# A routed expert FFN with run-time branches: more branches announced ahead, group work moved inside the arms, a one-hot made before the branch

## The chip, the core and the metric

The kernel runs on one core of a Trainium2 chip. The metric is the device time of one execution in microseconds (us), the median of three runs. TensorE (PE) does the matrix products, VectorE (DVE) and ScalarE (ACT) the element-wise work, and SyncE (SP) starts the loads of the expert weights.

## What is computed

One encoder layer over 256 tokens and 16 meta tokens of width 1024: two token mixers, a LayerNorm, then a feed-forward part in which each of the 256 tokens goes to 4 of 32 experts, then a LayerNorm. The change lies in the expert part alone:

```
def moe_ffn(x, ...):
    logits = x @ w_router + b_router
    top_val, top_idx = top_k(logits, 4)
    gates = softmax(top_val)
    # for each expert e, over the tokens that chose it:
    hidden = xb @ w_gate_up[e] + b_gate_up[e]            # 1024 -> 2048
    gate, up = hidden[:, :1024], hidden[:, 1024:]
    gate, up = minimum(gate, 7), clip(up, -7, 7)
    y = (gate * sigmoid(1.702 * gate) * (up + 1)) @ w_down[e] + b_down[e]
    # out[token] = sum over its 4 experts of gate_of_expert * y
```

How many tokens an expert gets is known only at run time.

## The kernel before

The mixers take the first 380 us or so. Then come the 32 experts in order, written out one behind the other in the program. The weights of an expert are 12 pages of 1 MB each, 8 of `w_gate_up` and 4 of `w_down`. They go through a ring of 19 buffers; SP starts the load of the page 19 places further on as soon as PE has used a page (`follow`), so a stall of PE ahead of such a use also delays a load.

An expert's work depends on its number of tokens n, which each engine loads into a register (`counts`). Three branches choose the arm: the outer one, labelled `x{e}` (n > 32), the inner one (n > 64), and inside that n > 96.

- The **small arm** (n up to 32): one part A, that is 8 steps of up products (L1098, with the bias at L1096), the activation on DVE and ACT (`act`, L1103 to L1111), two transposes (`turn`, L1117), 4 steps of down products (L1130), and the copy of the result into `yrow` (`place`, L1138 and L1140). 20 experts take it.
- The **mid arm** (33 to 64): parts A and B side by side. Seven experts take it: 7, 8, 14, 23, 25, 27 and 29.
- The **far arm** (65 and more): first `pick` makes a one-hot `eo` of the tokens past 64 (L1045), `gather` and `slots` use it (L1070, L1078, L1080), then come A and B and the further parts C and D. Experts 4, 6, 11, 20 and 30 take it.

In the program of PE an expert stands as: outer branch, inner branch, far arm, mid arm, small arm; behind the small arm is the place where all arms meet, called the landing here. The small arm runs straight into it; the far and the mid arm jump over what stands between. Behind the landing PE loads the next count (L1183) and comes to the next outer branch (L1192) and inner branch (L1193).

The tokens of four consecutive experts (a group, `GE` = 4) are gathered together. Between the landing of a group's last expert (e = 3, 7, 11, ...) and the next outer branch stand, in straight code, `gather_group` (L1055), and twice a `combine` (L1169, the previous group's rows into the sums `acc`) and a `slots` (L1078, L1080).

`tell` announces on PE the coming outer branch: an instruction that names the branch and says whether n > 32 there. It stands at the start of the small and the mid arm and behind the ups of A and B in the far arm.

## Time and profile before

| what | value |
|---|---|
| median of three runs | 1482.67 us (1479.99 to 1483.79) |
| the profiled execution, its own time | 1474.79 us |
| its span, first to last instruction | 1472.7 us |
| PE busy, share of the span | 1185.7 us, 81% |
| mean granted TensorE clock | 0.908 of full speed |
| DMA read over the span | 454.27 MB |

The profiled execution is 2.1 us longer than its span, and it is 0.5% below the median of the three runs. Times in the rows are counted from the start of the span; the expert part runs from about 381 us on. In a timeline row the first number is the start, the second the duration of a run of equal instructions, and the bracket at the end the idle time of the engine before them with what ended it; "issue" there means that no other engine or transfer that the profile shows ended it.

### The profile page before, as it was taken

To read this page: it belongs to the slowest core of one execution; us is meant where nothing else is said; L and a number is where in the kernel's file an instruction comes from. 1 tells how busy PE (TensorE), PEld (TensorE's weight loads), DVE (VectorE), ACT (ScalarE), POOL (GpSimd) and SP (SyncE) were. 2 spreads that over 40 slices of the span, in tenths; PEclk is the share of its full clock that TensorE was granted. 3 is DMA by queue.
4 is the path that set the end of the run, shared out by engine and by line. 5 is a ranking of instruction groups with operands and counts; after the bars stand their busy time and mean duration, and the time that the engine had idled before them with its cause. 6 is when DMAs were issued, how large, how long until landed. Compare 5 with 4: busy or idle time off the path is not lost. (4 is left out here: it accounts for less than half of the span.)

```text
span 1472.7 us, 24271 instructions
## 1 busy us (share of the span) xinstructions
PE 1185.7 (81%) x10294; PEld 727.6 (49%) x10294; DVE 426.1 (29%) x940; ACT 294.6 (20%) x630; POOL 83.0 (6%) x65
## 2 busy tenths in 40 slices
PE   5899999899777968688697976856976777787875
PEld 5799999889532533344243533411532443242432
DVE  5976765456411110211112012011021111111113
ACT  4454475454300100001000100100100010010011
POOL 5422400000100000000000000000000000000001
PEclk9999999999888999989888889977898898899888
DMA  6465673768499998877998399999998999999740
GB/s 170 133 168 125 153 185 106 225 200 332 182 405 417 418 412 354 347 301 302 377 418 325 151 416 418 415 418 418 419 382 350 416 417 416 417 416 414 307 174 31
DMA packets 101982, 458.40 MB, mean 311 GB/s; under 512 B 8626, under 2 KB 49739, under 8 KB 52635
## 3 DMA queue, kind: packets, MB, share of 16 engines
q1 hardware_dynamic: 100554, 451.59, 79.2%
q0 software_dynamic: 800, 3.03, 0.7%
q8 instruction: 146, 2.39, 0.7%
q10 hardware_dynamic: 400, 0.73, 0.2%
q14 instruction: 82, 0.66, 0.1%
HBM read 454.27 MB, written 1.05 MB: 309 GB/s over the span
## 5 line engine op out<-in xcount | busy, mean ns | idle before, releaser
L1098 PE MATMUL pA<-ring,w 128*32 128x512 f32 x2048 | 294.3, 664 | 21.7 <-DMA ring<-in_w_gate_up_dram 21.1
L1098 PEld LDWEIGHTS pA<-ring,w 128*32 128x32 f32 x2048 | 91.9, 120 | 170.9 <-issue 112.4
L1130 PE MATMUL dA<-ring,hd 128*32 128x256 f32 x2048 | 150.9, 443 | 17.4 <-ACT hd L1118 14.5
L1103 DVE TENSOR_SCALAR hd<-pA 128x256 f32<-128x256 f32 x32 | 13.6, 425 | 449.5 <-PE pA L1098 322.2
L1098 PE MATMUL pB<-ring,w 128*32 128x512 f32 x768 | 116.2, 618 | 0.0
L1130 PEld LDWEIGHTS dA<-ring,hd 128*32 128x32 f32 x2048 | 72.3, 126 | 79.8 <-issue 26.0
L1105 ACT ACTIVATE thA<-hd 128x256 f32<-128x256 f32 x32 | 13.3, 416 | 468.6 <-DVE hd L1103 455.0
L1140 DVE COPY yrow<-dA 32x256 f32<-32x256 f32 x96 | 40.4, 420 | 216.1 <-PE dA L1130 153.5
L1096 PE MATMUL pA<-bgt,sel 96*32 96x256 bf16 x256 | 19.4, 337 | 99.6 <-issue 93.2
L1096 PEld LDWEIGHTS <-sel 96*32 96x32 bf16 x400 | 12.8, 104 | 138.5 <-issue 124.5
L1055 PE MATMUL xg<-ext,hh 128*128 128x256 f32 x256 | 63.5, 410 | 8.7 <-issue 4.5
L1055 PEld LDWEIGHTS xg<-ext,hh 128*128 128x128 f32 x256 | 52.1, 206 | 21.2 <-issue 7.8
L1169 PE MATMUL acc<-yrow,pgb 128*128 128x512 f32 x128 | 58.1, 598 | 1.0 <-DVE yrow L1140 1.0
L1245 POOL DMA_DIRECT2D ring<-in_ln_g_dram x1 | 0.6, 574 | 1018.5 <-PE dB L1130 1018.5
L1098 PEld LDWEIGHTS pB<-ring,w 128*32 128x32 f32 x768 | 33.0, 116 | 46.9 <-issue 46.8
L1117 PE MATMUL atA<-ident,hd 128*128 128x128 f32 x64 | 16.0, 334 | 47.4 <-DVE hd L1111 47.4
L1138 ACT COPY yrow<-dA 32x256 f32<-32x256 f32 x32 | 11.6, 363 | 200.2 <-DVE yrow L1140 153.9
L1130 PE MATMUL dB<-ring,hd 128*32 128x256 f32 x768 | 51.6, 387 | 0.0
L1117 PEld LDWEIGHTS atA<-ident,hd 128*128 128x128 f32 x64 | 10.1, 207 | 78.2 <-issue 61.5
L1098 PE MATMUL pC<-ring,ext 128*32 128x512 f32 x320 | 39.7, 612 | 0.6 <-issue 0.6
L162 PE MATMUL xbc<-hTh,wh_xbc 128*128 128x272 f32 x128 | 38.2, 300 | 0.0
L163 PE MATMUL xbc<-hTl,wh_xbc 128*128 128x272 f32 x128 | 37.8, 296 | 0.0
(523 smaller groups left out, 2120.3 us busy)
## 6 DMA issues: line engine op xcount, KB each, us to landing
ring<-in_w_gate_up_dram SPq DMA_DIRECT2D x256, 1024.0 KB, 19.9
ring<-in_w_down_dram SPq DMA_DIRECT2D x127, 1024.0 KB, 19.5
wr_xbc<-in_w_in_dram SPq DMA_DIRECT2D x8, 1024.0 KB, 10.5
wr_g<-in_w_in_dram SPq DMA_DIRECT2D x8, 1024.0 KB
wr_z<-in_w_in_dram SPq DMA_DIRECT2D x4, 1024.0 KB
wr_k<-in_w_in_dram SPq DMA_DIRECT2D x4, 1024.0 KB, 10.9
wr_v<-in_w_in_dram SPq DMA_DIRECT2D x4, 1024.0 KB
wr_q<-in_w_in_dram SPq DMA_DIRECT2D x4, 1024.0 KB, 13.7
```

Source lines behind the costliest of these rows:

```text
L162: TE.matmul(p, wh, xh, start=first, stop=False)
L163: TE.matmul(p, wh, xl, start=False, stop=False)
L1055: TE.matmul(p[:, j, :], h1[:, b, k * 128:(k + 1) * 128], oh[:, b, :], start=b == 0, stop=b == 1)
L1096: TE.matmul(o[:, u, :], sel[:, e:e + 1].to_broadcast([96, 32]), bgt[u][:, 256 * j:256 * j + 256], start=u == 0, stop=False)
L1098: TE.matmul(o, x[:, k, :], w[:, :, 256 * j:256 * j + 256], start=False, stop=k == KD - 1)
L1103: V.tensor_scalar(gg, p[:, 0, :], 7.0, None, ALU.min)
L1105: A.activation(t, gg, AF.Tanh, scale=0.851)
L1117: TE.transpose(p[:, t, :], hd[:, co + 256 + t:co + 512:2], ident)
L1130: TE.matmul(p[j * 32:(j + 1) * 32, :], at[:, t, k * 32:(k + 1) * 32], w[:, t, j * 256:(j + 1) * 256], start=k == 0 and t == 0, stop=k == 3 ...
L1138: A.copy(o, p[r0:r0 + 32, :])
L1140: V.tensor_copy(o, p[j * 32:j * 32 + 32, :])
L1169: TE.matmul(ap[b][n], w[b], y[:, n * 512:(n + 1) * 512], start=False, stop=stop)
```

## The change

- A table `mid` holds for each expert 1 if n is up to 32 or over 64 and 0 from 33 to 64. Five DVE operations make it once, and PE loads an entry of it for each expert beside the count (L1182).
- The inner branch gets a label, `y{e}`, and `tell` announces it too, behind the outer one, with that entry as its direction. A third branch `z{e}` with an empty body is put at the landing and is named by `tell(True)` in the far and the mid arm. Its condition is `nz > S` with nz at most 1, so it can never hold, and the built program has neither this branch nor an announcement of it: PE has 186 announcements where there were 93, two in each place instead of one.
- `fill` puts the group work inside the arms, between ups and downs: both `combine` and `slots` into the group's first expert, `gather_group` into its last. Each arm has a copy of its own.
- `pick(e, 64)` runs ahead of the outer branch for every expert, and `eo` gets a fixed place in the tail of the buffer of `w1`.
- A second definition of `wps` with the same text is removed. Lines of the operations shift: downs from L1130 to L1127, `combine` from L1169 to L1166.

```
-        eo = wk.tile([128, NB, 64], F32, tag="sd", name=f"eo{name}")
         for b in range(NB):
             V.tensor_scalar(eo[:, b, :], iota[:, 0:64], float(off), posm[:, b, e:e + 1], ALU.add, ALU.is_equal)
-        return eo
...
+        pick(e, 64)
         with tc.If(n > 32, label=f"x{e}") as c1:
-            with tc.If(n > 64) as c2:
-                eo = pick(e, 64, f"{e}")
+            with tc.If(n > 64, label=f"y{e}") as c2:
                 gather(eo, f"x{e}")
                 slots(eo, slice(e, e + 1), pgx, f"x{e}")
                 ups(e, [pa, pb_], False)
-                tell()
+                tell(True)
...
             with c2.Else():
-                tell()
+                tell(True)
                 ups(e, [pa, pb_], True)
-                mark()
+                fill()
                 downs(e, [pa, pb_], True)
         with c1.Else():
-            tell()
+            tell(False)
             ups(e, [pa], True)
-            mark()
+            fill()
             downs(e, [pa], True)
+        with tc.If(nz > S, label=f"z{e}"):
+            pass
...
-            def mark(m=m, e=e):
+            def fill(e=e, g=g, el=el):
                 if e == 0:
                     start_acc()
                     V.memset(yx, 0.0)
+                if el == 0:
+                    for i in range(2):
+                        if e:
+                            combine(pgb[i], yrow[:, i])
+                        slots(oh[:, :, 128 * i:128 * i + 128], slice(g * GE, (g + 1) * GE), pgb[i], f"{'AB'[i]}{g}")
+                if el == GE - 1 and e + 1 < NE:
+                    gather_group(f"{g + 1}", range(0, 8, 2))
 
-            def tell(m=m, e=e):
+            def tell(far, m=m, e=e):
+                if far:
+                    tc.mark_branch_hint_location(f"z{e}", engines=[ET.PE])
                 if m is not None:
-                    tc.mark_branch_hint_location(f"x{e + 1}", hint=m > 32, engines=[ET.PE])
-
-            arms(e, n, mark, tell)
-            if el == GE - 1 and e + 1 < NE:
-                gather_group(f"{g + 1}", range(0, 8, 2))
-            if el == GE - 1 and e + 1 < NE or e == 0:
-                for i in range(2):
-                    if e:
-                        combine(pgb[i], yrow[:, i])
-                    h = g + 1 if e else 0
-                    slots(oh[:, :, 128 * i:128 * i + 128], slice(h * GE, (h + 1) * GE), pgb[i], f"{'AB'[i]}{h}")
+                    tc.mark_branch_hint_location(f"x{e + 1}", hint=m[0] > 32, engines=[ET.PE])
+                    tc.mark_branch_hint_location(f"y{e + 1}", hint=m[1], engines=[ET.PE])
```

On PE, at the border of experts 23 and 24, the program before has this behind the last downs (`dA`) of expert 23's small arm; the landing is the row behind the first branch:

```order
L1130 MATMUL dA_25726<-ring_3896,hd 32x256 x8
L1192 UNCONDITIONAL_BRANCH
L1055 MATMUL xg_25767<-ext,hh 128x256 x4
L1055 MATMUL xg_25773<-ext,hh 128x256 x4
L1055 MATMUL xg_25779<-ext,hh 128x256 x4
L1055 MATMUL xg_25785<-ext,hh 128x256 x4
L1169 MATMUL acc_3888<-yrow,pgb_3883 128x512
...
L1080 MATMUL ptB_25809<-gth,ext 128x4 x2
L1183 TENSOR_LOAD cnt
L1192 COMPARE_AND_BRANCH
L1193 COMPARE_AND_BRANCH
```

The changed kernel has at the same place, from the last ups of that arm on:

```order
L1098 MATMUL pA_26955<-ring_3933,w_3882 32x512 x4
L1055 MATMUL xg_27010<-ext,hh 128x256 x4
L1055 MATMUL xg_27016<-ext,hh 128x256 x4
L1055 MATMUL xg_27022<-ext,hh 128x256 x4
L1055 MATMUL xg_27028<-ext,hh 128x256 x4
L1117 MATMUL atA_27034<-ident,hd 128x128 x2
...
L1192 UNCONDITIONAL_BRANCH
L1181 TENSOR_LOAD cnt
L1182 TENSOR_LOAD mid
L1182 ISA x2
L1192 COMPARE_AND_BRANCH
L1193 COMPARE_AND_BRANCH
```

The gather stands between ups and transposes now, the `combine` rows have gone on into expert 24, and between the landing and the two branches only loads are left.

On DVE, ahead of the same two branches of expert 24, the program before has:

```order
L1183 TENSOR_LOAD cnt
L1192 COMPARE_AND_BRANCH
L1193 COMPARE_AND_BRANCH
L1045 TENSOR_SCALAR eo_25834<-iota,posm 128x64 x2
L1086 COPY gslx_25860<-ptx_25855 64x1
```

and the changed kernel:

```order
L1181 TENSOR_LOAD cnt
L1046 TENSOR_SCALAR w_3882<-iota,posm 128x64 x2
L1192 COMPARE_AND_BRANCH
L1193 COMPARE_AND_BRANCH
L1086 COPY gslx_27130<-ptx_27125 64x1
```

The two operations of `pick` moved from the far arm to a place ahead of both branches, and write into the buffer `w`.

## Rows read from the trace of the kernel before

**Rows 1.** Windows of the expert part; GB/s last, DMA share before it, granted clock before that

```profile
540.00:832.00 292.00, 229.98 (x2184) 112.60 (x2180) 44.38 (x123) 25.37 (x65) 0.00 (x0) 0.89 0.80 323
832.00:1032.00 200.00, 144.13 (x1278) 58.95 (x1274) 26.59 (x72) 13.59 (x34) 0.00 (x0) 0.85 1.00 414
1032.00:1472.00 440.00, 332.86 (x3064) 164.62 (x3052) 72.50 (x192) 43.44 (x101) 5.27 (x5) 0.89 0.85 347
```

**Rows 2.** Waits of PE over the span: total us, times, longest us

```profile
PE pA L1096 <- issue: 93.2, 16, 10.6
PE atA L1117 <- DVE hd L1111: 47.4, 26, 2.9
PE xgx L1070 <- DVE eo L1045: 10.4, 5, 3.1
```

**Rows 3.** Timeline of PE, where it last waits for pages, and of SP's page loads

```profile
467.13 1.94 PE L1098 MATMUL pA<-ring,w 128*32 128x512 f32 x8 [1.42 <-DMA ring<-in_w_gate_up_dram]
1031.62 1.07 PE L1130 MATMUL dA<-ring,hd 128*32 128x256 f32 x16 [0.76 <-DMA ring<-in_w_down_dram]
800.13 32.34 SPq L1002 DMA_DIRECT2D ring<-in_w_gate_up_dram  x3
```

**Rows 4.** The inner branch on PE's sequencer: ns min/median/max

```profile
L1193 PEldq COMPARE_BRANCH  x24: 65/3741/6758, 489.3 to 1422.1; - x24
```

**Rows 5.** Timeline of PE: first instruction of expert 10 and of experts 23, 27, 29, 7

```profile
725.45 0.47 PE L1096 MATMUL pA<-bgt,sel 96*32 96x256 bf16 x8 [0.58 <-DVE yrow L1140]
1149.68 0.68 PE L1096 MATMUL pA<-bgt,sel 96*32 96x256 bf16 x8 [5.64 <-issue]
1272.69 0.68 PE L1096 MATMUL pA<-bgt,sel 96*32 96x256 bf16 x8 [5.97 <-issue]
1344.38 0.68 PE L1096 MATMUL pA<-bgt,sel 96*32 96x256 bf16 x8 [5.70 <-issue]
630.01 0.68 PE L1096 MATMUL pA<-bgt,sel 96*32 96x256 bf16 x8 [10.63 <-issue]
```

**Rows 6.** Timeline of PE behind landings reached by a jump

```profile
706.80 0.68 PE L1096 MATMUL pA<-bgt,sel 96*32 96x256 bf16 x8 [9.12 <-issue]
1111.06 0.68 PE L1096 MATMUL pA<-bgt,sel 96*32 96x256 bf16 x8 [9.62 <-issue]
657.58 7.17 PE L1055 MATMUL xg<-ext,hh 128*128 128x256 f32 x32 [1.03 <-ACT yrow L1138]
805.70 7.16 PE L1169 MATMUL acc<-ext,pgx 64*128 64x512 f32 x8 [3.91 <-issue]
1182.74 5.23 PE L1055 MATMUL xg<-ext,hh 128*128 128x256 f32 x23 [1.30 <-issue]
1306.54 8.40 PE L1055 MATMUL xg<-ext,hh 128*128 128x256 f32 x31 [3.21 <-issue]
```

**Rows 7.** Timeline of PE: activation waits of a small and a mid arm

```profile
1137.71 0.48 PE L1117 MATMUL atA<-ident,hd 128*128 128x128 f32 x2 [2.04 <-DVE hd L1111]
1138.69 5.35 PE L1130 MATMUL dA<-ring,hd 128*32 128x256 f32 x64 [0.51 <-ACT hd L1118]
1167.39 0.48 PE L1117 MATMUL atA<-ident,hd 128*128 128x128 f32 x2 [1.14 <-DVE hd L1111]
1168.95 0.51 PE L1117 MATMUL atB<-ident,hd 128*128 128x128 f32 x2 [1.08 <-DVE hd L1111]
```

**Rows 8.** Timeline of PE ahead of expert 12, and ups at two clocks

```profile
822.46 3.60 PE L1169 MATMUL acc<-yrow,pgb 128*128 128x512 f32 x8
830.65 0.43 PE L1096 MATMUL pA<-bgt,sel 96*32 96x256 bf16 x8
725.66 7.12 PE L1098 MATMUL pA<-ring,w 128*32 128x512 f32 x64
707.18 9.67 PE L1098 MATMUL pA<-ring,w 128*32 128x512 f32 x64
```

**Rows 9.** The load of a count on PE's sequencer: ns min/median/max

```profile
L1183 PEldq TENSOR_LOAD <-cnt x32: 297/304/487, 388.0 to 1370.2; - x32
```

## The prediction

> **What bounds the kernel now.** I began with windows of the expert part, because the change touches nothing ahead of it but some small front work. The reader is to see three stretches [rows 1]. From 540 to 832 us the DMA engines are busy for 0.80 of the time and move 323 GB/s: the ring is full, loads wait for PE to use a page, and PE sets the pace. From 832 to 1032 the share is 1.00 at 414 GB/s: the loads set the pace. From 1032 on it is 0.85 at 347 GB/s, and PE sets the pace again. The timeline agrees: PE waits for pages around 467 us, and the last such wait ends at 1031.62; SP's three loads from 800.13 on stretch over 32.34 us, so the loads stop there until PE goes on [rows 3]. The path that sets the end is therefore PE from about 467 to 832, the loads from 832 to 1032, and PE from 1032 to the end. A microsecond saved on PE counts in the first and the last of these, and not in the middle.

> Next I read what PE waits for [rows 2]. By far the most stands at its first instruction of an expert (L1096): 93.2 us in 16 waits that nothing visible ended ("issue"). Behind that come 47.4 us ahead of the transposes, where PE waits for the activation, and 10.4 us in five waits for the one-hot of the far arm. These three are what the change is about.

> The 93.2 us look like code that isn't there yet when a branch lands. The inner branch is short at best, 65 ns, but its median is 3741 ns and its maximum 6758 ns [rows 4]. The outer branch is announced before: from small expert 9 to small expert 10 the jump goes over two whole arms and costs 0.58 us. Where the same small landing leads to a mid expert, the inner branch, not announced, jumps, and PE stands for 5.64, 5.97 and 5.70 us [rows 5]. Where the landing was itself reached by a jump, out of a mid or far arm, PE stands for 9.12 and 9.62 us although the outer branch had been announced [rows 6]: one fetch for the landing, one more for the arm.

> **The change part by part.**

> *Inner branch announced.* Experts 23, 27 and 29 are mid experts behind a small one in the last stretch: 5.64 + 5.97 + 5.70, each down to 0.58, saves 15.6 us [rows 5]. Expert 25 is alike, but its predecessor is the first of a group and its arm grows by the `combine` work between announcement and use; I count it at nothing, and at 5 more as the bound. Expert 7 follows a far expert and waits 10.63 us against 9.62 for a small expert in the same position [rows 5, 6], so its inner branch adds about 1.0 there: -1.0. Expert 14 lies in the stretch of the loads: nothing. The nothing-bound for all of this is rival C.

> *Landing announced.* The built program has no third announcement, so the jumps into the landing cost what they did.

> *Group work leaves the landing.* This speaks against the change. Behind the jump out of the last expert of a group stood straight code on PE, a gather of 7.17 us and the combines, under which the fetch of the next arm was hidden: ahead of experts 8, 12, 24 and 28 PE stood only 1.03, 3.91, 1.03 + 1.30 and 1.03 + 3.21 us (the 1.03 of the later two is the same wait as at 657.58) [rows 6]. Now two branches follow the landing at once, as they do at the 9.12 and 9.62 us. I take 9.12 behind the mid arms (7, 23, 27) and 9.62 behind the far arm (11): +8.1, +5.7, +6.8, +4.9 = +25.5 us. If only one fetch of 5.64 were exposed, it would be +11; with 10.63 at each, +31.

> [...]

> *Group work covers the activation.* In a small arm PE waits 2.04 us ahead of the transposes and 0.51 behind them, in a mid arm 1.14 and 1.08 [rows 7]. A gather or a combine of several us now lies in that place, on PE, while DVE and ACT finish. In the stretches that count these are experts 3, 19, 24 and 28 (small, 2.55 each) and 7, 8, 23 and 27 (mid, 2.22 each): -19.1 us. Far arms hide nearly all of it already behind their second half, and I count them at nothing. If DVE and ACT were held up by the copies and `slots` that come along, part of this would come back; the bound is half, +9.5.

> *One-hot ahead of the branch.* Five waits, 10.4 us [rows 2], all of them far experts in the stretches that count: -10.4. The two DVE operations run for every expert now, but DVE is busy for 44.38 of 292 us [rows 1], and reaches the landing ahead of PE. If `eo` in the buffer of `w1` waited for the previous users, that would be far experts' work long done: nothing.

> *Loads restart earlier.* `combine` and `slots` stand ahead of expert 12's ups from 822.46 to 830.65 us [rows 8], and the loads stand still meanwhile [rows 3]. Behind the ups they no longer delay the release of pages: -8.2, at the start of the stretch that the loads set.

> *Small things.* Another load of a register per landing, 0.304 us [rows 9], at some 21 landings that count: +6.4 if none is hidden; with the five small operations in front I take +6. The copies lengthen the code of all arms, so straight code crosses into code not yet there somewhat oftener: I choose +2, from one to two crossings of the 1.30 us that one cost inside a gather [rows 6].

> The clock: ups behind a long stall ran 9.67 us, without one 7.12 [rows 8], so 2.5 us hang on each stall. Three or four stalls vanish and four appear, so nothing is left.

> Sum: -15.6 - 1.0 + 25.5 - 19.1 - 10.4 - 8.2 + 6 + 2 = -20.8 us. The profiled execution took 1474.79, which makes 1454; it was itself 0.5% below the median of 1482.67, so the median after is forecast as 1482.67 - 20.8 = 1462.

> **The rivals.**

> *B, slower: the second announcement wipes out the first.* The two branches stand next to each other, and the trace of before never has two announcements open at once, so nothing there says that both are kept. If the later one wins, announced jumps to small arms behind small arms become full stalls: experts 10 and 22 lose 5.64 - 0.58 + 2.5 of clock = 7.6 us each, and 1, 2 and 3 as much again, of which I count half, since the ring hides some there: 15.2 + 11.4 = +26.6. The time is 1462 + 26.6 = 1488. For it: the announced gain is one of a single prefetch. Against it: an announcement names its own branch. It decides when these losses exceed 25 us.

> *C, no change: the inner announcement has no effect,* because it comes too late behind the first or because the outer branch's outcome supersedes it. The 16.6 us stay: 1462 + 16.6 = 1479. For it: the landing's jump already undoes an announced outer branch [rows 6]. Against it: behind a small arm there is no jump.

> *D: PE's gains end in page waits.* After 1032 the loads run at 0.85 share, so 15% of 440 us, 66 us, are spare [rows 1], against some 16 us net gained there (15.6 and 12.1 of covered activations and 4.1 of one-hots, less 11.7 at the landings of 24 and 28 and 4 of small things). I give it no more than a few us in the range.

> **How the numbers follow.** The forecast has 0.55, B 0.27, C 0.13, all else 0.05. Its own range is 1442 (the landing's lower bound, -14.5, and expert 25's 5) to 1474 (the upper bound +5.5 and a third of the uncovered activations). The range that should hold the time 8 times in 10 reaches on to B: 1442 to 1489. A measurement here can tell about 0.3%, 4.4 us, from no change: 0.53 of the forecast and half of C are faster, 0.60 in all; the other half of C, a third of B and the rest are the same, 0.18; the rest of B and mishaps are slower, 0.22.

> **What would show it.** Gaps under 1 us ahead of experts 23, 27 and 29 show the inner announcement right; 9 us ahead of 8, 12, 24 and 28 show the exposed landings; no wait for the activation in experts 3, 7, 8, 19, 23, 24, 27 and 28; no wait for `eo` at all; loads that restart some 8 us sooner behind expert 11. Stalls of 5 us ahead of experts 1, 2, 3, 10 and 22 would show B; unchanged stalls at 23, 27 and 29 show C. The forecast is most easily wrong in the landings: if the exposed stalls are as short as 5 us, the gain is nearly double; if the outer announcement fails at more places, it is gone.

## The result and the profile after

The changed kernel took 1526.45 us (median of 4 runs, 1520.13 to 1534.17) against 1482.73 us; the ratio is 1.031, with a 95% interval from 1.027 to 1.035. It is slower by 3.1%, where 1.4% faster was forecast and 1489 was the upper end of the range. The profiled execution has a span of 1529.7 us, so 57.0 us more than the one of before; that one was 8 us below its kernel's median and this one is 5 us above, so some 13 of the 57 are the choice of the two executions.

The waits of PE over the span, largest first (total us, times, longest):

```profile
PE pA L1096 <- issue: 167.9, 23, 12.5
PE atA L1117 <- DVE hd L1111: 28.7, 15, 3.0
PE dA L1127 <- ACT hd L1118: 13.8, 22, 0.9
PE xgx L1070 <- DVE w L1046: 12.0, 5, 3.1
PE pA L1098 <- issue: 9.0, 4, 3.9
```

Beside [rows 2]: the stalls ahead of an expert's first instruction grew from 93.2 us in 16 to 167.9 in 23, the wait for the activation fell from 47.4 to 28.7, the wait for the one-hot did not fall (10.4 to 12.0), and a wait is there that was not among the larger ones: stalls inside straight code of the ups, 9.0 us. Waits for pages are gone from the list; before, it had this:

```profile
PE pA L1098 <- DMA ring<-in_w_gate_up_dram: 21.1, 21, 1.5
```

The timeline of PE, first instruction of an expert; here small experts behind small ones (1, 2, 3, 10, 17, 22):

```profile
440.07 0.68 PE L1096 MATMUL pA<-bgt,sel 96*32 96x256 bf16 x8 [6.38 <-issue]
464.40 0.68 PE L1096 MATMUL pA<-bgt,sel 96*32 96x256 bf16 x8 [6.56 <-issue]
488.13 0.68 PE L1096 MATMUL pA<-bgt,sel 96*32 96x256 bf16 x8 [6.46 <-issue]
771.43 0.68 PE L1096 MATMUL pA<-bgt,sel 96*32 96x256 bf16 x8 [6.39 <-issue]
1010.49 0.68 PE L1096 MATMUL pA<-bgt,sel 96*32 96x256 bf16 x8 [7.85 <-issue]
1177.46 0.68 PE L1096 MATMUL pA<-bgt,sel 96*32 96x256 bf16 x8 [6.23 <-issue]
```

Each of them stands for 6 us and more; expert 10 waited 0.58 before [rows 5]. Mid experts behind small ones (14, 23, 29), and experts behind a group's end (8, 24, 28):

```profile
919.25 0.47 PE L1096 MATMUL pA<-bgt,sel 96*32 96x256 bf16 x8 [0.81 <-DVE yrow L1137]
1199.27 0.47 PE L1096 MATMUL pA<-bgt,sel 96*32 96x256 bf16 x8 [0.77 <-DVE yrow L1137]
1396.70 0.47 PE L1096 MATMUL pA<-bgt,sel 96*32 96x256 bf16 x8 [0.73 <-ACT yrow L1135]
...
704.08 0.68 PE L1096 MATMUL pA<-bgt,sel 96*32 96x256 bf16 x8 [7.93 <-issue]
1241.58 0.68 PE L1096 MATMUL pA<-bgt,sel 96*32 96x256 bf16 x8 [12.53 <-issue]
1374.17 0.68 PE L1096 MATMUL pA<-bgt,sel 96*32 96x256 bf16 x8 [9.85 <-issue]
```

The announced inner branch works: 23 and 29 waited 5.64 and 5.70 us before [rows 5], 0.77 and 0.73 now. The landings at a group's end are exposed as forecast ahead of 8, 24 and 28; ahead of 12 PE stands 3.19 us, where 9.62 was taken. The picture is that of rival B: mid experts behind small ones no longer stall, small ones do.

What ends such a stall can be read from the traces of both kernels. Transfers of the kind "instruction" have a queue of their own there (packets, MB, share), before and after:

```profile
q8 instruction: 146, 2.39, 0.7%
q8 instruction: 157, 2.57, 0.7%
```

In each of the 50 waits of PE by "issue" of 2 us and more (19 before, 31 after) such a transfer, of 16 KB, ends, and PE goes on 1.3 to 2.4 us behind the last one. In the kernel before, the 9.12 us of [rows 6] hold two, begun at 697.97 and 703.80, and the 5.64 us ahead of expert 23 one, at 1146.73. For the announced jump to expert 10 one was over at 723.58, ahead of PE's wait of 0.58 us; ahead of expert 24 one began at 1186.37, under the gather and the `combine`, and expert 24 began without a wait. "Fetch" stands for these transfers here; whose code they carry the profile doesn't say.

The windows of the same stretches as [rows 1], the last up to the end of this execution (granted clock, DMA share, GB/s at the end):

```profile
540.00:832.00 292.00, 226.10 (x2123) 109.64 (x2116) 44.36 (x129) 22.26 (x59) 0.00 (x0) 0.88 0.79 320
832.00:1032.00 200.00, 145.19 (x1352) 71.48 (x1350) 30.17 (x90) 17.91 (x46) 0.00 (x0) 0.86 0.90 367
1032.00:1529.00 497.00, 363.17 (x3324) 172.85 (x3324) 81.83 (x229) 44.97 (x106) 5.27 (x5) 0.85 0.84 342
```

In the middle stretch the DMA share fell from 1.00 to 0.90: PE, not the loads, sets the pace there now.

### The profile page after: what moved, and what is told of

Its sections match the earlier page's. It is cut to its first block, busy times and chain, and to the rows that moved or that the text cites. A ratio compares the mean times of both kernels' runs of the same rounds, so it can differ in the third digit from the quotient of the medians.

```text
span 1529.7 us, 24478 instructions
## 1 busy us (share of the span) xinstructions
PE 1198.8 (78%) x10294; PEld 740.2 (48%) x10294; DVE 437.3 (29%) x999; ACT 294.0 (19%) x630; POOL 82.8 (5%) x65
## 5 line engine op out<-in xcount | busy, mean ns | idle before, releaser
L1098 PE MATMUL pA<-ring,w 128*32 128x512 f32 x2048 | 311.9, 702 | 9.0 <-issue 9.0
L1098 PEld LDWEIGHTS pA<-ring,w 128*32 128x32 f32 x2048 | 99.1, 129 | 169.7 <-issue 159.7
L1096 PE MATMUL pA<-bgt,sel 96*32 96x256 bf16 x256 | 21.1, 387 | 170.9 <-issue 167.9
L1127 PE MATMUL dA<-ring,hd 128*32 128x256 f32 x2048 | 136.5, 411 | 13.8 <-ACT hd L1118 13.8
L1098 PE MATMUL pB<-ring,w 128*32 128x512 f32 x768 | 117.0, 611 | 2.0 <-issue 2.0
L1096 PEld LDWEIGHTS <-sel 96*32 96x32 bf16 x400 | 13.2, 106 | 215.2 <-issue 196.1
L1127 PEld LDWEIGHTS dA<-ring,hd 128*32 128x32 f32 x2048 | 66.7, 118 | 68.0 <-ACT hd L1118 19.2
L1055 PE MATMUL xg<-ext,hh 128*128 128x256 f32 x256 | 60.3, 396 | 1.2 <-DVE ext L1039 1.2
L1166 PE MATMUL acc<-yrow,pgb 128*128 128x512 f32 x128 | 58.9, 604 | 1.0 <-DVE yrow L1137 1.0
L1098 PEld LDWEIGHTS pB<-ring,w 128*32 128x32 f32 x768 | 34.2, 116 | 50.2 <-issue 47.4
L1127 PE MATMUL dB<-ring,hd 128*32 128x256 f32 x768 | 51.2, 386 | 0.0
L1098 PE MATMUL pC<-ring,ext 128*32 128x512 f32 x320 | 42.8, 667 | 2.5 <-issue 2.5
L162 PE MATMUL g<-hTh,wh_g 128*128 128x256 f32 x128 | 37.6, 294 | 2.8 <-ACT wh_g L183 2.7
L1070 PE MATMUL xgx<-w,hh 128*128 128x64 f32 x160 | 28.0, 357 | 13.3 <-DVE w L1046 12.0
L1117 PE MATMUL atA<-ident,hd 128*128 128x128 f32 x64 | 15.8, 333 | 28.7 <-DVE hd L1111 28.7
## 6 DMA issues: line engine op xcount, KB each, us to landing
ring<-in_w_down_dram SPq DMA_DIRECT2D x127, 1024.0 KB, 10.8
```

What stands on the lines that cost most here:

```text
L162: TE.matmul(p, wh, xh, start=first, stop=False)
L1055: TE.matmul(p[:, j, :], h1[:, b, k * 128:(k + 1) * 128], oh[:, b, :], start=b == 0, stop=b == 1)
L1070: TE.matmul(p[:, k, :], h1[:, b, k * 128:(k + 1) * 128], eo[:, b, :], start=b == 0, stop=b == 1)
L1096: TE.matmul(o[:, u, :], sel[:, e:e + 1].to_broadcast([96, 32]), bgt[u][:, 256 * j:256 * j + 256], start=u == 0, stop=False)
L1098: TE.matmul(o, x[:, k, :], w[:, :, 256 * j:256 * j + 256], start=False, stop=k == KD - 1)
L1117: TE.transpose(p[:, t, :], hd[:, co + 256 + t:co + 512:2], ident)
```

## The experiments

| kernel | us | ratio to before, 95% interval |
|---|---|---|
| x_only | 1498.42 | 1.009 to 1.019 |
| y_then_x | 1508.00 | 1.014 to 1.027 |
| xy_landing | 1504.92 | 1.013 to 1.026 |
| x_landing | 1500.37 | 1.009 to 1.018 |
| pick_only | 1480.94 | 0.996 to 1.002 |
| pad16, pad32, pad48 | 1492.46, 1485.62, 1476.95 | 1.005 to 1.016, 1.001 to 1.006, 0.996 to 1.001 |
| fill_only | 1494.30 | 1.004 to 1.017 |
| one_landing | 1501.18 | 1.009 to 1.018 |
| x_twice | 1519.38 | 1.024 to 1.033 |
| one_fill, again as one_fill_b | 1473.69, 1479.58 | 0.991 to 1.001, 0.997 to 1.003 |
| one_fill_pad48 | 1487.91 | 1.004 to 1.011 |
| one_half, one_half_pad32 | 1478.35, 1474.20 | 0.996 to 1.001, 0.993 to 0.999 |

**Outer announcement alone.**

```
-                    tc.mark_branch_hint_location(f"y{e + 1}", hint=m[1], engines=[ET.PE])
```

> The changed kernel without the announcement of the inner branch; all else stays. Theory L (PE keeps one announcement, and the later one replaces the earlier, so the inner branch's wipes out the outer branch's): the stalls of 6 us ahead of experts 1, 2, 3, 10, 13, 18, 19 and 22 fall under 1 us, those of 5.6 us ahead of the mid experts 14, 23, 27 and 29 come back, the stalls of 8 to 12 us ahead of 8, 12, 24 and 28 stay; 1484 us (1475 to 1495), about 40 below the changed kernel. Rival G (the loss comes from the group work inside the arms: longer code and landings without cover): the stalls ahead of 1, 2, 3, 10 and 22 stay, at least 1515 us.

It took 28 us less than the changed kernel, and the stalls ahead of 1, 3, 10, 16, 17 and 18 fell to some 0.5 us or less, those of 2 and 22 to 1.9, of 13 and 19 to 3.5 and 3.1 (at 2, 19 and 22 PE waits for DVE there), while 14, 23, 27 and 29 stand 6.2 to 6.5 us again. That is L's pattern; G as the whole cause is out. 18 us over before stay; 1498 lies above the 1475 to 1495 that L had expected.

**The order of the two turned round.**

```
+                    tc.mark_branch_hint_location(f"y{e + 1}", hint=m[1], engines=[ET.PE])
                     tc.mark_branch_hint_location(f"x{e + 1}", hint=m[0] > 32, engines=[ET.PE])
-                    tc.mark_branch_hint_location(f"y{e + 1}", hint=m[1], engines=[ET.PE])
```

> The changed kernel with the two announcements in the other order: inner branch first, outer branch last. Theory L: the outer one is kept now; as the kernel with the outer announcement alone, stalls ahead of the mid experts 23, 27 and 29 back at 5.6 us, none ahead of 1, 2, 3, 10 and 22; 1485 us, within 8 of that kernel. Rival N (two open announcements cancel each other whatever their order): 6 us ahead of both kinds, about 1540 us. Rival K (each branch has its own announcement, and the order matters not): as the changed kernel, about 1526 us.

Small experts 1, 2, 3, 10 and 22 wait 0.6 to 0.8 us, mid ones 23, 27 and 29 some 6.5: the last one named is the one that works, so neither N nor K holds. But 17 stalls 6.34 us, and the time is 10 above x_only, where no more than 8 was expected.

**The same code, with the second announcement repeating the first.**

```
-                    tc.mark_branch_hint_location(f"y{e + 1}", hint=m[1], engines=[ET.PE])
+                    tc.mark_branch_hint_location(f"x{e + 1}", hint=m[0] > 32, engines=[ET.PE])
```

> The changed kernel, as many instructions at the same places, but the second announcement in each arm repeats the outer branch instead of naming the inner one. Theory L (the later announcement replaces the earlier): 1498 us as with one announcement, stalls ahead of 1, 2, 3, 10, 13, 18, 19 and 22 mostly under 2 us, those of the mid experts 5.6 to 6.5. Rival T (two announcements cost in themselves, whatever they name): about 1526 us, stalls of 6 us ahead of the small experts. Rival M (moved code made the difference): in between, stalls at other places.

PE has as many instructions at the same places as in the changed kernel. The timeline of PE, experts 1, 2, 10, 22 and then 23 and 29:

```profile
432.20 0.47 PE L1096 MATMUL pA<-bgt,sel 96*32 96x256 bf16 x8 [0.73 <-ACT yrow L1135]
449.75 0.47 PE L1096 MATMUL pA<-bgt,sel 96*32 96x256 bf16 x8 [0.74 <-DVE yrow L1137]
759.59 0.47 PE L1096 MATMUL pA<-bgt,sel 96*32 96x256 bf16 x8 [0.64 <-DVE yrow L1137]
1151.87 0.38 PE L1096 MATMUL pA<-bgt,sel 96*32 96x256 bf16 x5 [0.63 <-DVE yrow L1137]
1179.00 0.68 PE L1096 MATMUL pA<-bgt,sel 96*32 96x256 bf16 x8 [6.33 <-issue]
1392.11 0.68 PE L1096 MATMUL pA<-bgt,sel 96*32 96x256 bf16 x8 [6.59 <-issue]
```

On equal code the name in the second announcement decides which branches stall, as L forecast. That PE holds a single announcement is L's reading of this; the runs show the stalls alone. One expert does not fit: 17 stalls 6.30 us here and 6.34 in y_then_x, though its branch is the last one named; this stays unexplained. And the time is 1519 and not 1498: L's expectation missed, and T's number is nearer though its stalls are not there.

y_then_x is equal code too, and its stalls ahead of first instructions are nearly those of x_twice (128.4 us against 130.6). Its experts 10 and 23:

```profile
749.61 0.47 PE L1096 MATMUL pA<-bgt,sel 96*32 96x256 bf16 x8 [0.62 <-DVE yrow L1137]
1165.76 0.68 PE L1096 MATMUL pA<-bgt,sel 96*32 96x256 bf16 x8 [6.57 <-issue]
```

So naming the outer branch last instead of the inner one is worth 7 us net by x_twice and 18 by y_then_x, with intervals of the two that overlap. It is that little because the mid experts stall again in both. The 21 us between x_twice and x_only come with 93 fewer instructions on PE, whose removal moves all code behind. Of the 30.8 us between the spans of their profiled executions, 18.2 are longer busy time of PE on the same 10294 matmuls (1202.2 against 1184.0 us, at a mean granted clock of 0.885 against 0.901); the rest are waits.

**Both announcements, group work back behind the landing; and the same with the outer one alone.**

```
-                if el == 0:
...
-                if el == GE - 1 and e + 1 < NE:
-                    gather_group(f"{g + 1}", range(0, 8, 2))
...
+            if el == GE - 1 and e + 1 < NE:
+                gather_group(f"{g + 1}", range(0, 8, 2))
```

> The changed kernel with its group work back behind the landing: both announcements and the early one-hot stay. Theory L: the small experts behind small ones stall 6 us, the mid ones 23, 27 and 29 do not, 8, 12, 24 and 28 stand 1 to 4 us as before the change; 1482.7 + 18 (experts 1 to 3) + 11 (10, 13) + 6 (22) - 15 (23, 27, 29) + up to 12 (17 to 19) = 1508 us (1495 to 1520). Rival G: the announcements alone gain, 1465 us.

> The kernel before with the one-hot made ahead of the branch and the extra load of a register per expert, one announcement, group work behind the landing. The forecast's step on the one-hot: waits of 10.4 us gone, 1475 us. Rival P (PE waits there for DVE, which is still copying the previous result, so an earlier place in the code changes nothing): five waits of 1 to 3 us stay, and with the extra loads 1485 us, no change from before.

The pair differs by 4.5 us. In xy_landing experts 1, 2, 3, 10 and 22 stand 5.6 to 6.5 us, and 14, 23, 25 and 29 under 1.7: L again, gains and losses nearly even. The surprise was x_landing, 20 us above before though it only moves `pick` and loads one more table entry per expert.

**Only the early one-hot.**

```
+        pick(e, 64)
         with tc.If(n > 32, label=f"x{e}") as c1:
             with tc.If(n > 64) as c2:
-                eo = pick(e, 64, f"{e}")
```

> The kernel before with the one-hot made ahead of the outer branch and nothing else; PE's program has as many instructions as before. Forecast of the prediction: 10 us faster, 1471. Theory P (PE waits there for DVE, which comes late to the branch because it still copies the last result): the five waits of 1 to 3 us ahead of the gather stay, 1481 us, no change, and so the 20 us of the kernel with early one-hot and table loads come from those loads or from the moved code.

No change, and the five waits stay, 10.1 us. Theory P's forecast holds: DVE comes to the branch late. In the changed kernel, ahead of expert 20, DVE first and then PE:

```profile
1079.49 1.32 DVE L1137 COPY yrow<-dA 32x256 f32<-32x256 f32 x3 [9.90 <-PE dA L1127]
1080.85 0.42 DVE L1046 TENSOR_SCALAR w<-iota,posm 128x64 f32<-128x64 f32 x2
```

```profile
1075.76 3.66 PE L1127 MATMUL dA<-ring,hd 128*32 128x256 f32 x64 [0.72 <-ACT hd L1118]
1081.25 3.15 PE L1070 MATMUL xgx<-w,hh 128*128 128x64 f32 x23 [1.82 <-DVE w L1046]
```

The copies of the last downs hold DVE until 1080.81, then `pick` runs; PE ended its downs at 1079.42 and waits 1.82 us for it. Ahead of 6, 11 and 30 (2.2, 3.1 and 3.1 us) copies of the last result hold DVE before the change too. Ahead of 4 and 20 it was the landing's `slots` then (1.02 and 1.01 us), and the copies took their place when the group work moved. Expert 20 before, DVE and PE:

```profile
1048.50 0.42 DVE L1045 TENSOR_SCALAR eo<-iota,posm 128x64 f32<-128x64 f32 x2 [0.40 <-DVE gd4B L1084]
1048.90 1.30 PE L1070 MATMUL xgx<-eo,hh 128*128 128x64 f32 x10 [1.01 <-DVE eo L1045]
```

**Code moved, nothing more executed.**

```
                 with tc.If(n > 96) as c3:
                     ups(e, [pc, pd_], True)
+                    if e == 0:
+                        for _ in range(16):
+                            TE.matmul(ap[0][0], pgx[0], yx[:, 0:512], start=False, stop=False)
```

The added matmuls stand in an arm that expert 0 doesn't take; pad32 and pad48 have 32 and 48 of them.

> The kernel before with 16 matmuls (64 instructions on PE) added in the arm for more than 96 tokens of expert 0, which these inputs never run: nothing more is executed, but all code behind stands 64 instructions further on. Theory M (what a branch costs depends on where its code falls, so adding code moves stalls): single gaps ahead of an expert's first instruction change by 2 to 6 us, and the time moves by 5 to 20 us in one direction or the other: 1470 to 1500. Rival E (only executed instructions cost): 1481 us, within 4 of the kernel before, gaps unchanged.

> The same with 32 matmuls, 128 instructions. Theory M: other gaps than with 64, 1470 to 1500 us, and the kernels with 0, 64, 128 and 192 lie over 10 us apart from lowest to highest. Rival E: 1481 us.

> The same with 48 matmuls, 192 instructions. Theory M: again other gaps, 1470 to 1500 us. Rival E: 1481 us.

1476.95 to 1492.46 us, 15.5 apart: theory M. Two of the waits of PE in pad16:

```profile
PE pA L1096 <- issue: 95.2, 14, 11.1
PE pA L1098 <- issue: 11.0, 5, 3.0
```

The stalls in straight code (L1098) are 11.0 us where before they were nothing of size, and expert 26 stands 11.07 us where it stood 6.77. In pad48 it is 7.88, in pad32 9.33. So x_landing's 20 us can come from its 96 more instructions in the places they fall, and from running them; the two were not separated.

**Only the group work moved.**

```
+                if el == GE - 1 and e + 1 < NE:
+                    gather_group(f"{g + 1}", range(0, 8, 2))
...
-            if el == GE - 1 and e + 1 < NE:
-                gather_group(f"{g + 1}", range(0, 8, 2))
```

(`combine` and `slots` likewise.)

> The kernel before with the group work inside the arms and nothing else: no inner announcement, no early one-hot, no table. The prediction's terms as far as they hold: landings +25.5, activations covered -19.1, loads restarted -8.2, straight crossings +2: 1479 us, no change, and 10 either way for where the code falls. Rival: only the covered activations count, 1455 us.

1494, above the 1479 expected, with 8, 24 and 28 standing 9.5, 9.6 and 6.3 us and the activation waits as low as in the changed kernel. Part of it lies ahead of the expert part (below).

**One announcement, chosen at run time.**

```
+                    with tc.If(m[1] > 0) as ch:
+                        tc.mark_branch_hint_location(f"x{e + 1}", hint=m[0] > 32, engines=[ET.PE])
+                    with ch.Else():
+                        tc.mark_branch_hint_location(f"y{e + 1}", hint=m[1], engines=[ET.PE])
```

> One announcement per arm, chosen at run time: a small branch on PE over the table entry of the next expert runs either the outer branch's announcement (next expert small or far) or the inner one's (next expert mid). Group work behind the landing, one-hot early. Theory L (one announcement is kept, the last): gaps under 1.3 us ahead of both the small experts 1, 2, 3, 10 and 22 and the mid ones 14, 23, 27 and 29; against the kernel with the outer announcement alone in the same arrangement (1500) 5 us less at each of 23, 25, 27 and 29, so 1480 us, and 10 either way for where the code falls. Rival S (the small branch itself costs a fetch of 3 to 6 us in many arms): 1500 us or more.

> The changed kernel, group work inside the arms, with the one announcement chosen at run time. Theory L: against the kernel with the outer announcement alone and group work inside the arms (1498) some 18 less, 1480 us, and 10 either way; against the changed kernel (1526) over 30 less, because neither the stalls of the small experts nor those of the mid ones are left. Rival S: 1498 us or more.

> The version with one announcement chosen at run time and group work inside the arms, once more: 1474 us, 0.3 to 0.5% below the kernel before.

> The same version with 48 matmuls (192 instructions) added in expert 0's arm for more than 96 tokens, which is not run. If its gain does not hang on where code falls: 1474 us, within 5. By theory M: 1465 to 1490, single stalls at other experts.

In one_fill, the changed kernel with this edit alone, 53 us of its 1526 are gone. The waits of PE there:

```profile
PE pA L1096 <- issue: 102.2, 17, 11.3
PE atA L1117 <- DVE hd L1111: 28.7, 15, 3.0
```

That is in line with L: with one announcement that names the branch that will jump, both kinds mostly lose their stall (1 to 3 at 0.8 to 1.6 us, 14, 25 and 29 under 1, but 10 stands 4.6, 16 and 17 3.7 and 3.5, and 22, 23 and 27 some 3.3). At 23 and 27 it is no branch that ends the wait but `pick` on DVE (`w`, L1046), which now stands ahead of every expert: three such waits, 9.2 us. Yet the second timing is even with the kernel before, and with the code moved by 192 instructions it is 0.7% slower: it beats the changed kernel, not the one before. In one_landing the choice brought nothing against x_landing (1501 and 1500): 37 us less stand ahead of first instructions, but other waits of the expert part grew by 28, up to 9.85 us at one place, ahead of part C of expert 4. That is rival S's number; of its mechanism this place alone may be an instance, since the choice stands just ahead of it (3.73 us there in the kernel before, but 4.17 in one_fill with the same choice).

**The gather alone back behind the landing.**

```
-                if el == GE - 1 and e + 1 < NE:
-                    gather_group(f"{g + 1}", range(0, 8, 2))
...
+            if el == GE - 1 and e + 1 < NE:
+                gather_group(f"{g + 1}", range(0, 8, 2))
```

> One announcement chosen at run time, combine and slots inside the arms of a group's first expert, but the gather back behind the landing of its last. If the gather covers the fetch of the next arm: the stalls ahead of experts 8, 24 and 28 (5.6, 8.9 and 11.3 us with the gather in the arm) fall to 1 to 5 us, while the activation waits of experts 3, 7, 19, 23 and 27 come back (2.2 to 2.6 each): some 8 us less than the version with the gather in the arm, 1470 us, and 10 either way for where code falls. Rival: the fetch of the landing itself stands ahead of the gather, and only moves: 1478 us or more.

> The same with 32 matmuls (128 instructions) added in expert 0's arm for more than 96 tokens, which is not run: within 5 of the unpadded one if where code falls matters little for it, otherwise up to 15 away, with single stalls at other experts.

No gap ahead of 8 and 12, 4.2 and 5.0 us ahead of 24 and 28: with the gather behind the landing, less stands ahead of 8, 24 and 28 than the 5.6, 8.9 and 11.3 us with it in the arm, but the landing's own stall now stands ahead of the gather of expert 8 (4.96 us at 670.61), so part of it only moved. 1478 and 1474 us; the second has an interval just below 1 (0.993 to 0.999), the best version found, by less than code positions alone have moved the time.

## Why the prediction was wrong

Its steps against the two profiled executions (us, after less before):

| step | forecast | measured |
|---|---|---|
| inner announcement, at mid experts | -16.6 (7, 23, 27, 29) | -19.6 (14, 23, 27, 29) |
| outer announcement lost | 0; rival B +26.6 | +56.0 (1, 2, 3, 10, 13, 16 to 19, 22) |
| landings of 8, 12, 24, 28, with the `combine` ahead of 12 | +25.5 | +27.6 |
| activation covered | -19.1 | -20.0 (all waits for `hd` in the expert part) |
| one-hot | -10.4 | +1.6 |
| stalls in straight code of the ups (L1098) | +2 | +12.4 |
| waits for pages | not a term | -24.1 |
| ahead of the expert part (4.2 idle, 5.6 PE busy) | within +6 | +9.8 |
| PE busy in the expert part, with the same matmuls (835.6 to 843.1) | nil | +7.5 |

These sum to 51.2 of the 57.0; of the rest 3.9 stand ahead of expert 26 (6.77 before, 10.62 now). The loads' earlier restart (-8.2) has no line, since the loads no longer bound the stretch behind it.

- The failing step is "inner branch announced", which let both announcements stand. The outer one's loss stood at 0 in the sum; it measured 56.0 us of stalls, less the 24.1 of page waits that went, so some 32 us, the largest single part of the miss. Rival B had this loss, at a chance of 0.27, and the runs show it on equal code (x_twice, y_then_x). They give up the inner gain of 19.6 as well, which leaves some 12 of the 32; they showed 7 and 18.
- B's price failed too. It counted experts 10 and 22 and half of 1 to 3, and nothing between 832 and 1032 us, as time there counted for nothing. Experts 13 and 16 to 19, all in that stretch, stalled 5 to 6 us more each. The loads had only 20.0 us of PE's waits to give there; the rest came through, and the stretch became PE's. A stretch's slack is an amount, and the sum of new stalls has to be held against it. Experts 16 and 17 before, and 16 now:

```profile
933.96 0.43 PE L1096 MATMUL pA<-bgt,sel 96*32 96x256 bf16 x8
951.23 0.47 PE L1096 MATMUL pA<-bgt,sel 96*32 96x256 bf16 x8 [1.57 <-DVE yrow L1140]
980.04 0.68 PE L1096 MATMUL pA<-bgt,sel 96*32 96x256 bf16 x8 [6.24 <-issue]
```

- The one-hot: the wait carried DVE's name, and the prediction took the place of `pick` for its cause. The cause was DVE's work ahead of it, copies at 6, 11 and 30 and `slots` at 4 and 20. "DVE reaches the landing ahead of PE" was wrong; DVE's timeline there would have shown it.
- Landings and activation were right in size as sums, and nearly cancel. One row was misread: the 3.91 us of [rows 6] (5.73 after) stand ahead of the far arm's own `combine`, still inside the arm of expert 11, and not behind the landing; the landing ahead of expert 12 showed 3.19.
- Straight code: the stall was named, its size wrong. +2 was taken from one or two stalls of 1.30 us; single ones here reach 3.89. Moving code alone moves the time by up to 15.5 us between kernels that execute the same, so for a change that moves this much code a forecast finer than that has little to stand on. The fetch ahead of the 1.30 us of [rows 6] ended 1.41 us before PE went on, and of the 9.0 us after the change the three largest stalls (2.17, 2.79 and 3.89 us) each have one that ended 1.51, 1.31 and 1.42 us before.
- The clock was put at nil, because stalls were to balance. They did not: the mean granted clock is 0.881 where it was 0.908, and the expert part's same matmuls took 7.5 us longer.
- What stays open: the 40 us between the kernel before and x_twice are seen in rows (landings, straight code, front, clock), but how far each is the edit itself or where the code fell was not separated.

## What to carry to other kernels

Announce one branch at a time on PE, the one that will jump; of two side by side here it was the branch named second that was spared the stall (expert 1: 6.38 us with the inner one second, 0.73 with the outer one; expert 23: 0.77 and 6.33). Before taking straight code away from behind a jump, look at what the fetch of the next arm hides under: ahead of expert 24 it was the gather and the `combine`, with waits of 1.03 and 1.30 us, and without them 12.53 us stand there. Where taken branches stall as here, try an edit with the code moved, by instructions in an arm that isn't run, before believing a gain or loss of 1%.

## What was not expected of the hardware

Code that is never executed changed the time: 192, 64 and 128 instructions in front gave ratios of 0.999, 1.011 and 1.003.

The stalls inside straight code end at a nearly fixed distance from the start of an arm. In the changed kernel, first instruction and stall of experts 22 and 27:

```profile
1177.46 0.68 PE L1096 MATMUL pA<-bgt,sel 96*32 96x256 bf16 x8 [6.23 <-issue]
1182.78 1.93 PE L1098 MATMUL pA<-ring,w 128*32 128x512 f32 x8 [2.17 <-issue]
1328.20 0.44 PE L1096 MATMUL pA<-bgt,sel 96*32 96x256 bf16 x4 [0.72 <-DVE yrow L1137]
1333.33 1.01 PE L1098 MATMUL pA<-ring,w 128*32 128x512 f32 x1 [3.89 <-issue]
```

They begin 3.2 and 1.2 us behind the arm's first instruction and end 5.3 and 5.1 us behind it. Over the 18 profiles, 72 of the 78 such stalls of more than 0.5 us in parts A and B end 4.8 to 6.1 us behind it, wherever they begin. It looks as if the code further on came some 5 us after the arm is entered, and as if its position decided how long the code at hand lasts until then. In these two a fetch ends 3.81 and 3.71 us behind the arm's first instruction, 1.51 and 1.42 us before PE goes on. The rest is a reading of the traces; no run tried it.

In the kernels with group work inside the arms, the load of the gate and up bias, well ahead of the expert part, came later. Waits of ACT in the changed kernel, where before they were 8.9 and 7.1 us:

```profile
ACT wh_g L183 <- DMA wr_g<-in_w_in_dram: 12.0, 2, 7.6
ACT bgt L846 <- DMA bgr<-in_b_gate_up_dram: 10.6, 1, 10.6
```

In x_only, fill_only and one_fill the second is 10.8, 10.6 and 9.8, and so it is in one_half (10.8), which has only `combine` and `slots` inside; in x_landing, xy_landing, pick_only, pad16 and pad48 it is 6.8 to 7.1. The expert part's first gather starts some 8 us later in the former (390.4 to 393.6 us) than in the latter (382.4 to 383.9); pad32 and one_landing lie between (386.7 and 386.3). The cause was not tried.
